# Two memory tiles for the modulation rows, gate blocks of layer 1 loaded in layer 1, a longer warm-up, the last projection in three column ranges, a new order table

## The chip, the core and the metric

One core of one Trainium2 chip runs the whole program. The metric is the device time of one execution in microseconds (us); lower is better. TensorE (PE) multiplies and has a queue of weight loads of its own (PEld in the profile), VectorE (DVE) and ScalarE (ACT) do the elementwise work, and SyncE (SP) issues nearly all transfers (DMA).

## The reference

One inference step with two layers over 640 tokens (512 latent, 128 context), width 1024, all in float32:

```
h = RMSNorm(x) * (1 + scale) + shift      # shift, scale, gate = SiLU(cond) @ ada_w[l] + ada_b[l]
u = h @ w_in[l]                           # one input projection for four head groups
A: differential attention   B: gated short convolution
C: latent attention         D: neighbourhood attention
y = concat(group_out * SiLU(z)) @ w_out[l]
x = x + gate * y                          # after layer 1: final RMSNorm
```

Context and latent tokens have different conditions, so shift, scale and gate exist twice (s = 0, 1). The keys and values of the context tokens are outputs too.

## The kernel before

Activations lie with the 1024 features on partitions, as eight blocks of 128 by 640 tokens. To keep float32 accuracy every product is done three times: an operand is split into an upper and a lower part (`whi`, `wlo` of a weight, `hh`, `hl` of an activation block), and upper by upper, upper by lower and lower by upper are summed in a PSUM bank. Each matmul instruction has its own load of 128 by 128 weights, even where the next one multiplies with the same weights: the trace has 5570 of both.

The code records operations into a plan (class `Plan`). `schedule` (L325) goes over them with a price for each and picks, for each engine, the one that can start first; ties go by a number, the place in the program plus `SHIFT[group]`. The table `SHIFT` so sets the order within each engine's queue. All instructions are emitted from one line, L464; the profile therefore goes by tile names.

The stages, in order of time:

- **Start.** `keep_warm(WARM[0])` puts dummy matmuls of 128 columns (`bank<-ones`) at the head of PE. Eight modulation blocks of layer 0 follow (`ada_first`, L611): each loads two halves of `adaw` (512 KB each) into buffers that are used for other things later (`yt`, `adst`, `qs`, `ks`, `bias`, `hl`), multiplies them with the condition `cs` (four matmuls of 32 columns of weights by 256 for a half, 8 records in the trace), copies the result to `adasb` (ACT), sums it with two tiny matmuls (`bank<-par,adasb`), and DVE writes `modB` and `modA` of that block. `keep_warm(WARM[1..4])` puts dummies behind the first four halves. Next to it runs the RMS norm of the first 384 columns: eight squares on ACT, seven sums on DVE, one matmul with `ones` by 384 columns, Ln and Exp on ACT, then `t<-cst,thi` on DVE. `finish` (L690) scales a block by `modA` and `modB` on ACT and splits it into `hh` and `hl`, with which the input projection `tm_chunk(0, "a")` (L700) begins: per block 5 token tiles by 3 products by 512 columns.
- **Middle.** Projections and attention of layer 0. In between, `ada_next` takes the other sixteen modulation blocks (four gate blocks of layer 0, all twelve of layer 1) one by one: two loads into `wraw`, matmuls, copy, and two small transfers into the DRAM tile `adram`; `ada_end` (L638) reads them back, sums them and writes `modA`, `modB`, `modG`. In the code before, all sixteen are done in layer 0. Then layer 0's output projection and layer 1 in the same manner.
- **Output projection.** `HALVES[l]` cuts the 640 columns into ranges; the loop at L1330 goes over them. For each range, eight output blocks (`fb`) take 24 matmuls each: 8 input blocks by 3 products. The split weights stay in `whi`/`wlo`, `adst`, `qs`/`ks` and `yt` for all ranges. DVE adds `gate * acc` to the old x (`cst<-bank,modG,...`), ACT squares the block (`thi`, `tlo`) and multiplies it by the norm weight. In layer 1 the end of a range is: last sum, square, matmul with `ones`, Ln, Exp, two products with 1/rms on DVE, two transfers to `yt`.

```
HALVES = (((0, 384), (384, 640)), ((0, 384), (384, 640)))   # L26: before, layer 0 and layer 1
WARM = (15, 10, 8, 4, 4)                                    # L36
for hf, (c0, c1) in enumerate(HALVES[l]):                   # L1330
    for n, kt in enumerate(YK):
        PE.matmul(acc[:, :w], wh[:, kt], hh[kt][:, c0:c1], ...)
        PE.matmul(acc[:, :w], wh[:, kt], hl[kt][:, c0:c1], ...)
        PE.matmul(acc[:, :w], wl[:, kt], hh[kt][:, c0:c1], ...)
```

Of the kernel before, what the change touches and what calls it, by code (L numbers as in the profile page):

```python
# [21 lines left out]
L = 2  # L22
X1 = (4, 4, 4, 4, 4, 4, 4, 4)
WA = (2, 6, 11, 16)
LATE = (16, 17)
HALVES = (((0, 384), (384, 640)), ((0, 384), (384, 640)))  # L26
# [9 lines left out]
WARM = (15, 10, 8, 4, 4)  # L36
SHIFT = {"": 38, "a0": 47, "a1": -28, "ada0": -8588, "av0": 6296, "av1": 3, "b0": 25951, "b1": 24557, "c0": -2462, "d0": 62, "d1": 33941, "f0.0": -174, "f0.1": 22, "f1.0": -183, "f1.1": 2841, "h0.0": -4317, "h0.1": 205, "h1.0": 7, "h1.1": -10499, "h10.0": 1418, "h10.1": -8, "h11.0": 638, "h11.1": 4686, "h2.0": -3351, "h2.1": -22079, "h3.0": -2855, "h4.0": -2974, "h4.1": -2909, "h5.0": -1, "h5.1": -9, "h6.0": 797, "h6.1": -6113, "h7.0": 20, "h7.1": 13278, "h8.0": 5300, "h9.0": -7596, "lam": 6901, "o0.0": -505, "o1.0": -80, "o1.1": 26, "p0.0": 162, "p0.1": -20, "p2.0": -2125, "p2.1": 432, "p3.0": -1337, "p3.1": 4371, "p4.0": -1388, "p4.1": -27369, "p7.0": -1727, "p7.1": 960, "p8.1": -18800, "pa0": 51, "pa1": -552, "qk00": -18970, "qk01": 10605, "qk10": 10903, "qk11": 14623, "x0": -3000, "x1": 6892, "x2": -1536, "y0": -1625, "y1": 9425, "y2": -77, "z0": -13, "z1": -227}
FILL = (('z', 4), ('d', 6), ('qk0', 7), ('qk1', 8), ('b', 12))
D = 1024
NT = 640  # L40
# [442 lines left out]
def body(ctx: ExitStack, tc: tile.TileContext, i, o):  # L483
# [68 lines left out]
    for op in R.ops[-WARM[0]:]:  # L552
        op.cost = {"PE": 320}
# [9 lines left out]
    adram = R.tile([L, 12, 2, 4, 256], F32, name="adram", space="dram")  # L563
# [6 lines left out]
    def wpiece(l, name, idx):  # L570
        if l == 0 and name == "a":
            at(WA[idx])
            R.offset += WBOOST
        else:
            R.offset = 0
        off, kk, n = PIECES[name][idx]
        src = i["win"][l, off:off + 128 * kk * n].rearrange("(p c) -> p c", p=128)
        return wsplit(src, kk, n)
# [19 lines left out]

    def ada_rows(l, blk, raws, warm):
# [24 lines left out]

    def ada_block(l, blk):
# [8 lines left out]
        for s in range(2):  # L634
            SP.dma_start(adram[l, blk, s], sb[s:97 + s:32])
        R.need, R.group = need, group

    def ada_end(l, b0, b1_):  # L638
# [3 lines left out]
        tag, n = ("wraw", 1024) if l == 0 else ("bias", BIAS_W)  # L642
        rows = R.tile([128, n], F32, name=tag, tag=tag, bufs=3 if l == 0 else 1)[0:m, 0:1024]
        SP.dma_start(rows, adram[l, b0:b1_].rearrange("b s k c -> (b s) (k c)"))
# [5 lines left out]
        v = pt[:, 0:2 * m].rearrange("p (c b s) -> p b c s", c=2, b=nb)  # L650
        wide = lambda t, n: t[:, :, None].to_broadcast([128, n, 2])
        if nb == 12:
# [3 lines left out]
        for c in range(2):  # L656
            V.tensor_add(modG[:, l, c:8:2], v[:, nb - 4:nb, c], wide(sp[:, l, 16 + c:24:2], 4))
        R.group = group

    later = [(0, b) for b in range(8, 12)] + [(1, b) for b in range(12)]  # L660

    def ada_next(l):

        if l == 0 and later:
            ll, blk = later.pop(0)
            ada_block(ll, blk)
            if blk == 11:
                ada_end(ll, 8 if ll == 0 else 0, 12)
                gate[0] = len(R.ops) - 1
# [166 lines left out]
    for l in range(L):  # L836
        if l == 0:
# [359 lines left out]
        def fill_d():  # L1197
# [5 lines left out]
            ada_next(l)  # L1203
# [4 lines left out]
        def fill_qk(p):  # L1208
# [15 lines left out]
            ada_next(l)  # L1224
# [10 lines left out]
            ada_next(l)  # L1235
# [91 lines left out]
        c0, c1 = HALVES[l][1]  # L1327
        xall = R.tile([128, 2816], F32, name="xall", tag="hl")[:, :8 * (c1 - c0)].rearrange("p (k c) -> p k c", k=8)
        SP.dma_start(xall, xsrc[:, :, c0:c1].rearrange("k p c -> p k c"))
        for hf, (c0, c1) in enumerate(HALVES[l]):  # L1330
            R.group = f"o{hf}.{l}"
            xn = xns[hf]
            for fb in range(8):
# [5 lines left out]
                if hf:  # L1339
                    xo = xall[:, fb]  # L1340
# [17 lines left out]
            rstd = rms_rows(xn, (0, 7, 8) if l + 1 == L and hf == 1 else (0, 8))  # L1358
# [126 lines left out]
```

## Time and profile before

| | us |
|---|---|
| median of 3 runs | 825.73 (825.54 to 825.94) |
| profiled execution | 825.87 |
| its span in the profile | 824.1 |
| PE busy | 799.7 (97%), 5570 matmuls |
| PEld busy | 746.0 (91%) |
| DVE / ACT busy | 578.9 (70%) / 505.0 (61%) |
| mean granted TensorE clock | 0.992 of full |

The 1.8 us between the profiled execution's time and its span lie outside what the trace covers. A matmul's record is longer than the room it takes, since matmuls overlap; what one costs is the distance from its start to the next start. PEclk is the clock that was granted to TensorE: 1.00 is 2.4 GHz, 0.50 is 1.2 GHz.

### The profile page before, as it was taken

How to read it: one execution, taken by the hardware profiler on the slowest of the kernel's cores; microseconds unless marked ns; L12 is line 12 of the kernel's file. 1: busy time of each engine (PE TensorE's matmuls, PEld its weight loads, DVE VectorE, ACT ScalarE, POOL GpSimd, SP SyncE). 2: the span in 40 equal slices, each digit the busy share in tenths (PEclk: the TensorE clock that was granted, in tenths of full speed). 3: DMA queues.
4: the chain of work that ended last, by engine and by line, in shares of the span. 5: the costliest groups of instructions: out<-in, count | busy, mean ns of one | idle time of the engine just before them, and what ended most of it. 6: DMA issues, size and time to landing. Idle time of an engine off the chain costs nothing.

```text
span 824.1 us, 14974 instructions
## 1 busy us (share of the span) xinstructions
PE 799.7 (97%) x5570; PEld 746.0 (91%) x5570; DVE 578.9 (70%) x1296; ACT 505.0 (61%) x1108; POOL 0.2 (0%) x4
## 2 busy tenths in 40 slices
PE   7999999998999999999999999999999999999995
PEld 6789898998898888989998899999999989999995
DVE  3744499798674985837367636986987899876643
ACT  5852487677883874624237436866887878645432
POOL 0000000000000000000000000000000000000000
PEclk8999999999999999999999999999999999999998
DMA  9924533444562787756650355333146646823221
GB/s 313 364 100 109 169 88 83 114 133 119 173 162 83 186 259 203 254 170 215 238 193 30 89 139 165 105 79 104 61 108 159 145 106 184 254 70 90 84 77 52
DMA packets 50029, 120.15 MB, mean 146 GB/s; under 512 B 7940, under 2 KB 21892, under 8 KB 49956
## 3 DMA queue, kind: packets, MB, share of 16 engines
q1 hardware_dynamic: 49812, 119.11, 48.2%
q8 instruction: 44, 0.72, 0.4%
q14 instruction: 29, 0.24, 0.1%
q10 hardware_dynamic: 144, 0.07, 0.0%
HBM read 82.69 MB, written 6.59 MB: 108 GB/s over the span
## 4 chain that ended last, share of the span: by engine, by line
PE 85%; ACT 5%; DVE 4%; DMA 3%; issue 1%; SPq 1%; DVEq 0%; ACTq 0%
PE bank L464 81%; PE pair L464 5%; ACT t L464 2%; ACT thi L464 1%; DVE t L464 1%; DMA wraw<-adaw 1%; DMA bias<-bias 1%; DVE tlo L464 1%; DMA yt<-adaw 1%; SPq L464 1%; DVE mn L464 1%; DMA q<-hl 0%; DVE cst L464 0%; ACT avt L464 0%; DVE adasb L464 0%
## 5 line engine op out<-in xcount | busy, mean ns | idle before, releaser
L464 PE MATMUL bank<-hh,whi 128*128 128x320 f32 (+2 forms) x640 | 202.2, 317 | 0.3 <-ACT adasb L464 0.3
L464 PE MATMUL bank<-hh,wlo 128*128 128x320 f32 (+2 forms) x640 | 201.0, 315 | 0.0
L464 PE MATMUL bank<-hl,whi 128*128 128x320 f32 (+2 forms) x640 | 200.7, 314 | 0.0
L464 PEld LDWEIGHTS bank<-hh,whi 128*128 128x128 f32 x640 | 120.5, 188 | 2.8 <-issue 1.2
L464 PEld LDWEIGHTS bank<-hh,wlo 128*128 128x128 f32 x640 | 120.3, 188 | 2.4 <-issue 1.6
L464 PEld LDWEIGHTS bank<-hl,whi 128*128 128x128 f32 x640 | 120.6, 188 | 2.1 <-issue 1.2
L464 DVE TENSOR_TENSOR wlo<-wraw,whi 128x1024 fp32r<-128x1024 f32 (+1 forms) x64 | 76.5, 1195 | 62.8 <-ACT whi L464 62.5
L464 ACT ACTIVATE thi<-bank 128x512 fp32r<-128x512 f32 (+3 forms) x164 | 76.8, 486 | 49.1 <-PE bank L464 45.4
L464 PE MATMUL bank<-whi,hl 128*128 128x256 f32 (+2 forms) x320 | 105.9, 332 | 0.0
L464 PE MATMUL bank<-whi,hh 128*128 128x256 f32 (+2 forms) x320 | 105.1, 333 | 0.7 <-DVE adst L464 0.5
L464 PE MATMUL bank<-wlo,hh 128*128 128x256 f32 (+2 forms) x320 | 105.1, 329 | 0.0
L464 DVE TENSOR_TENSOR tlo<-bank,thi 128x512 fp32r<-128x512 f32 (+3 forms) x164 | 86.8, 548 | 16.9 <-ACT thi L464 16.1
L464 ACT ACTIVATE whi<-wraw 128x1024 fp32r<-128x1024 f32 (+1 forms) x64 | 66.3, 1035 | 51.9 <-PE bank L464 40.6
L464 DVE TENSOR_REDUCE mn<-pair 128x1 f32<-128x640 f32 x96 | 77.9, 816 | 7.0 <-PE pair L464 4.4
L464 ACT ACTIVATE t<-pair,mn 128x640 f32<-128x640 f32 x96 | 75.9, 792 | 9.2 <-DVE mn L464 6.1
L464 PE MATMUL bank<-par,t 128*128 128x128 f32 x456 | 79.6, 274 | 1.4 <-DVE tlo L464 1.4
L464 PE MATMUL pair<-ks,qs 96*128 96x320 f32 (+1 forms) x256 | 62.9, 327 | 4.6 <-ACT t L464 4.3
L464 PEld LDWEIGHTS bank<-whi,hh 128*128 128x128 f32 x320 | 60.1, 189 | 6.6 <-issue 0.8
L464 PE MATMUL bank<-thi,vs 128*128 128x256 f32 (+3 forms) x224 | 64.3, 295 | 0.8 <-ACT t L464 0.8
L464 PEld LDWEIGHTS bank<-whi,hl 128*128 128x128 f32 x320 | 60.3, 188 | 5.1 <-issue 1.6
L464 PEld LDWEIGHTS bank<-wlo,hh 128*128 128x128 f32 x320 | 60.4, 189 | 5.0 <-issue 1.2
L464 PE MATMUL bank<-tlo,vs 128*128 128x256 f32 (+3 forms) x224 | 64.0, 303 | 0.5 <-DVE tlo L464 0.5
(191 smaller groups left out, 1450.7 us busy)
## 6 DMA issues: line engine op xcount, KB each, us to landing
wraw<-win SPq DMA_DIRECT2D x52, 512.0 KB, 4.1
wraw<-adaw SPq DMA_DIRECT2D x32, 512.0 KB, 4.8
ks<-hl SPq DMA_DIRECT2D x48, 192.0 KB, 3.6
wraw<-wout SPq DMA_DIRECT2D x16, 512.0 KB, 3.9
bias<-bias SPq DMA_DIRECT2D x8, 896.0 KB, 6.8
ks<-hl SPq DMA_DIRECT2D x48, 96.0 KB, 2.2
qs<-hl SPq DMA_DIRECT2D x48, 80.0 KB, 2.1
qs<-hl SPq DMA_DIRECT2D x24, 160.0 KB, 2.5
```

The lines of the kernel that those rows point to most:

```text
L464: done = getattr(engines[op.engine], method)(*[fix(x) for x in args], **{k: fix(x) for k, x in kw.items()})
```

## The change

- `HALVES` of layer 1: three ranges, 384, 128 and 128 columns, in place of 384 and 256. The old x for columns 384 to 640 is still loaded in one transfer (`xall`).
- `WARM`: 34 dummies at the head instead of 15, then 4, 4, 4, 4 instead of 10, 8, 4, 4. The first weight piece's load moves ahead (`WA` 0, 5, 10, 15).
- At the start the second half of block 0's modulation is made to wait for the norm's matmul (`second`, `R.rooted`), the first weight piece's split comes behind the norm, and `modB`/`modA` come earlier on DVE (priority 3000 lower).
- `adram` becomes two tiles, one for each condition s; `ada_end` reads each in a transfer of its own.
- The four gate blocks of layer 1 move from layer 0 to layer 1 (`later` has two lists, and `fill_b` of layer 1 takes from the second); blocks 0 to 7 of layer 1 end in an `ada_end` of their own in layer 0.
- A new `SHIFT` table: nearly every group has another number, so the order changes in all queues.

```
-HALVES = (((0, 384), (384, 640)), ((0, 384), (384, 640)))
+HALVES = (((0, 384), (384, 640)), ((0, 384), (384, 512), (512, 640)))
-WARM = (15, 10, 8, 4, 4)
-SHIFT = {"": 38, "a0": 47, "a1": -28, "ada0": -8588, ...
+WARM = (34, 4, 4, 4, 4)
+SHIFT = {"": 38, "a0": 44, "a1": -51, "ada1": 1198, ...
...
-    adram = R.tile([L, 12, 2, 4, 256], F32, name="adram", space="dram")
+    adram = [R.tile([L, 12, 4, 256], F32, name=f"adram{s}", space="dram") for s in range(2)]
...
+        if l == 0 and name == "a" and idx == 0:
+            R.ops[split_at].deps.add(R.rooted)
...
+            if warm and blk == 0:
+                second.append(len(R.ops))
...
+        for op in R.ops[-2:]:
+            op.prio -= 3000
...
-            SP.dma_start(adram[l, blk, s], sb[s:97 + s:32])
+            SP.dma_start(adram[s][l, blk], sb[s:97 + s:32])
...
-        SP.dma_start(rows, adram[l, b0:b1_].rearrange("b s k c -> (b s) (k c)"))
+        for s in range(2):
+            SP.dma_start(rows[s * nb:s * nb + nb], adram[s][l, b0:b1_].rearrange("b k c -> (b) (k c)"))
...
-    later = [(0, b) for b in range(8, 12)] + [(1, b) for b in range(12)]
+    later = ([(0, b) for b in range(8, 12)] + [(1, b) for b in range(8)], [(1, b) for b in range(8, 12)])
...
+                if n == 0:
+                    R.rooted = len(R.ops) - 1
...
+                    if n == 0 and "PE" in op.calls:
+                        for k in range(4):
+                            R.ops[second[1] + k].deps.add(op.n)
...
-                    xo = xall[:, fb]
+                    xo = xall[:, fb, c0 - HALVES[l][1][0]:c1 - HALVES[l][1][0]]
...
-            rstd = rms_rows(xn, (0, 7, 8) if l + 1 == L and hf == 1 else (0, 8))
+            rstd = rms_rows(xn, (0, 7, 8) if l + 1 == L and hf == 2 else (0, 8))
```

PE's queue at the very start, before. `ones` are the dummies, `yt,cs` halves of modulation blocks, `t_112,ones` the norm's matmul, `par_62,adasb` the small sums, `whi,hh` the first real matmuls:

```order
L464 MATMUL bank<-ones 128x128 x15
L464 MATMUL bank<-yt,cs 32x256 x4
L464 MATMUL bank<-ones 128x128 x4
L464 MATMUL bank<-yt,cs 32x256 x4
L464 MATMUL bank<-ones 128x128
L464 MATMUL bank<-t_112,ones 128x384
L464 MATMUL bank<-par_62,adasb 128x2 x2
L464 MATMUL bank<-yt,cs 32x256 x8
```

The same place in PE's queue after the change:

```order
L464 MATMUL bank<-ones 128x128 x34
L464 MATMUL bank<-yt,cs 32x256 x4
L464 MATMUL bank<-ones 128x128 x4
L464 MATMUL bank<-t_118,ones 128x384
L464 MATMUL bank<-yt,cs 32x256 x4
L464 MATMUL bank<-ones 128x128 x3
L464 MATMUL bank<-par_62,adasb 128x2 x2
L464 MATMUL bank<-yt,cs 32x256 x4
```

The norm's matmul moves ahead of the second half of block 0. From the first `yt,cs` to the last dummy of the start there stand 26 dummies before and 16 after; a row of nine of them, which stood behind the first block's `whi,hh` matmuls, is gone.

PE's queue in layer 1's output projection where the first range ends, before:

```order
L464 MATMUL bank<-hh_536,yt 128x384
L464 MATMUL bank<-hl_542,yt 128x384
L464 MATMUL bank<-hh_536,yt 128x384
L464 MATMUL bank<-hh_203,whi 128x256
L464 MATMUL bank<-hl_222,whi 128x256
L464 MATMUL bank<-hh_203,wlo 128x256
L464 MATMUL bank<-hh_245,whi 128x256
```

The same place after:

```order
L464 MATMUL bank<-hh_558,yt 128x384
L464 MATMUL bank<-hl_570,yt 128x384
L464 MATMUL bank<-hh_558,yt 128x384
L464 MATMUL bank<-hh_213,whi 128x128
L464 MATMUL bank<-hl_237,whi 128x128
L464 MATMUL bank<-hh_213,wlo 128x128
L464 MATMUL bank<-hh_261,whi 128x128
```

192 matmuls of 256 columns become 384 of 128 columns. They stand in one unbroken row to the end of the program, but for the four matmuls with `ones`; no longer matmul stands between them.

## Rows read from the trace of the kernel before

**Rows 1.** The page: busy time of the engines, share of the span, instructions.
```profile
PE 799.7 (97%) x5570; PEld 746.0 (91%) x5570; DVE 578.9 (70%) x1296; ACT 505.0 (61%) x1108; POOL 0.2 (0%) x4
```

**Rows 2.** Stages: window, length, busy of PE, PEld, DVE, ACT, POOL; clock, DMA.
```profile
10.70:20.80 10.10, 10.09 (x76) 6.71 (x76) 3.58 (x9) 4.31 (x9) 0.00 (x0) 0.73 1.01 381
...
100.00:420.00 320.00, 311.70 (x2275) 286.73 (x2274) 234.35 (x530) 204.55 (x459) 0.00 (x0) 1.00 0.56 166
...
790.50:814.20 23.70, 23.70 (x198) 23.40 (x196) 11.34 (x25) 8.75 (x18) 0.00 (x0) 1.00 0.19 68
```

**Rows 3.** The start: start, duration, instruction, idle before; last, landings (issues, KB, median us).
```profile
1.05 5.93 PE L464 MATMUL bank<-ones 128*128 128x128 f32 x30 [1.05 <-DVE ones L464]
10.71 1.08 PE L464 MATMUL bank<-yt,cs 128*32 128x256 f32 x8 [3.74 <-DMA yt<-adaw]
11.72 2.08 PE L464 MATMUL bank<-ones 128*128 128x128 f32 x8
15.33 1.23 PE L464 MATMUL bank<-t,ones 128*128 128x384 f32 x2
16.39 0.50 PE L464 MATMUL bank<-par,adasb 128*128 128x2 f32 x4
20.26 0.64 PE L464 MATMUL bank<-yt,cs 128*32 128x256 f32 x8
20.83 0.96 PE L464 MATMUL bank<-whi,hh 128*128 128x512 f32 x3
23.01 2.17 PE L464 MATMUL bank<-ones 128*128 128x128 f32 x18
28.64 1.61 SPq L464 DMA_DIRECT2D hl<-adaw  x2
42.87 1.07 PE L464 MATMUL bank<-hl,cs 128*32 128x256 f32 x16
...
wraw<-win SPq DMA_DIRECT2D x6, 512.0 KB, 9.8
```

**Rows 4.** Weight loads, then matmuls, of 128 columns in succession.
```profile
340.81 0.19 PEld L464 LDWEIGHTS bank<-thi,vs 128*128 128x128 f32 x1
340.92 0.19 PEld L464 LDWEIGHTS bank<-tlo,vs 128*128 128x128 f32 x1
341.03 0.19 PEld L464 LDWEIGHTS bank<-hh,wlo 128*128 128x128 f32 x1
...
340.86 0.28 PE L464 MATMUL bank<-thi,vs 128*128 128x128 f32 x1
340.98 0.27 PE L464 MATMUL bank<-tlo,vs 128*128 128x128 f32 x1
341.09 0.36 PE L464 MATMUL bank<-hh,wlo 128*128 128x320 f32 x1
```

**Rows 5.** PE: two 128-column matmuls behind a longer one, then others.
```profile
226.88 0.34 PE L464 MATMUL bank<-ks,qs 128*128 128x128 f32 x2
227.06 0.27 PE L464 MATMUL bank<-k,q 128*128 128x128 f32 x1
```

**Rows 6.** The 256-column range: first and last of its 192 matmuls, then the ending.
```profile
790.54 0.28 PE L464 MATMUL bank<-hh,whi 128*128 128x256 f32 x1
...
792.80 0.81 PE L464 MATMUL bank<-thi,ones 128*128 128x384 f32 x2
...
813.85 0.28 PE L464 MATMUL bank<-hh,yt 128*128 128x256 f32 x1
814.17 0.61 DVE L464 SCALAR_TENSOR_TENSOR cst<-bank,modG,hl 128x128 f32<-128x128 f32 x2 [1.29 <-PE bank L464]
815.28 0.70 PE L464 MATMUL bank<-tlo,ones 128*128 128x256 f32 x2 [0.72 <-ACT tlo L464]
816.97 2.36 DVE L464 TENSOR_TENSOR cst<-cst,thi 128x1024 f32<-128x1024 f32 x2 [2.19 <-ACT thi L464]
818.23 1.55 SPq L464 DMA_DIRECT2D yt<-cst  x2
```

More of the change, by code (lines that the diff above doesn't have):

```diff
@@ L23 @@
 X1 = (4, 4, 4, 4, 4, 4, 4, 4)
-WA = (2, 6, 11, 16)
+WA = (0, 5, 10, 15)
 LATE = (16, 17)
-HALVES = (((0, 384), (384, 640)), ((0, 384), (384, 640)))
+HALVES = (((0, 384), (384, 640)), ((0, 384), (384, 512), (512, 640)))
 START = ((0, 384), (384, 640))
@@ L551, in body @@
     keep_warm(WARM[0])
-    for op in R.ops[-WARM[0]:]:
-        op.cost = {"PE": 320}
+    for n, op in enumerate(R.ops[-WARM[0]:]):
+        op.cost = {"PE": 340 if n < 14 else 215}
     modA = R.tile([128, L, 8, 2], F32, name="modA")
@@ L577, in wpiece @@
         src = i["win"][l, off:off + 128 * kk * n].rearrange("(p c) -> p c", p=128)
-        return wsplit(src, kk, n)
+        split_at = len(R.ops) + 1
+        w = wsplit(src, kk, n)
+        if l == 0 and name == "a" and idx == 0:
+            R.ops[split_at].deps.add(R.rooted)
+        return w
     def wsplit(src, kk, n, place=None):
@@ L597, in at @@
         R.offset = ada_at[min(h, 15)] + 7.5 * max(h - 15, 0) + 0.5 - len(R.ops)
+    second = []
     def ada_rows(l, blk, raws, warm):
@@ L641, in ada_end @@
         m = 2 * nb
-        tag, n = ("wraw", 1024) if l == 0 else ("bias", BIAS_W)
-        rows = R.tile([128, n], F32, name=tag, tag=tag, bufs=3 if l == 0 else 1)[0:m, 0:1024]
-        SP.dma_start(rows, adram[l, b0:b1_].rearrange("b s k c -> (b s) (k c)"))
+        tag, n = ("wraw", 1024) if nb == 4 else ("bias", BIAS_W)
+        rows = R.tile([128, n], F32, name=tag, tag=tag, bufs=3 if nb == 4 else 1)[0:m, 0:1024]
+        for s in range(2):
+            SP.dma_start(rows[s * nb:s * nb + nb], adram[s][l, b0:b1_].rearrange("b k c -> (b) (k c)"))
         su = R.tile([128, 256], F32, name="adasb", bufs=1)[0:m]
@@ L649, in ada_end @@
             PE.transpose(pt[:, m * c:m * c + m], su[:, 128 * c:128 * c + 128], ident[0:m, 0:m])
-        v = pt[:, 0:2 * m].rearrange("p (c b s) -> p b c s", c=2, b=nb)
+        v = pt[:, 0:2 * m].rearrange("p (c s b) -> p b c s", c=2, b=nb)
         wide = lambda t, n: t[:, :, None].to_broadcast([128, n, 2])
-        if nb == 12:
+        if nb == 8:
             V.tensor_add(modB[:, l], v[:, 0:8, 0], wide(sp[:, l, 0:8], 8))
@@ L655, in ada_end @@
             V.tensor_mul(modA[:, l], modA[:, l], wide(sp[:, l, 24:32], 8))
-        for c in range(2):
-            V.tensor_add(modG[:, l, c:8:2], v[:, nb - 4:nb, c], wide(sp[:, l, 16 + c:24:2], 4))
+        for c in range(2 if nb == 4 else 0):
+            V.tensor_add(modG[:, l, c:8:2], v[:, :, c], wide(sp[:, l, 16 + c:24:2], 4))
         R.group = group
-    later = [(0, b) for b in range(8, 12)] + [(1, b) for b in range(12)]
+    later = ([(0, b) for b in range(8, 12)] + [(1, b) for b in range(8)], [(1, b) for b in range(8, 12)])
     def ada_next(l):
-        if l == 0 and later:
-            ll, blk = later.pop(0)
+        if later[l]:
+            ll, blk = later[l].pop(0)
+            gate[1] = l
             ada_block(ll, blk)
-            if blk == 11:
-                ada_end(ll, 8 if ll == 0 else 0, 12)
-                gate[0] = len(R.ops) - 1
+            if blk in (7, 11):
+                ada_end(ll, 0 if blk == 7 else 8, blk + 1)
+                if l == 0:
+                    gate[0] = len(R.ops) - 1
     def rms_rows(xv, cuts=(0, 8), wide=False):
@@ L1202, in fill_d @@
             R.need = dst.ops[0]
-            ada_next(l)
+            if l == 0:
+                ada_next(l)
             tm_seq(l, "dv", ev_d)
@@ L1223, in ev_q @@
                 V.scalar_tensor_tensor(lo, acc, 0.125, hi.bitcast(F32), op0=OP.mult, op1=OP.subtract)
-            ada_next(l)
+            if l == 0:
+                ada_next(l)
             fm_mm(wh, wl, ev_q)
@@ L1234, in ev_k @@
                     SP.dma_start(o["sdk"][l, p], st)
-            ada_next(l)
+            if l == 0:
+                ada_next(l)
             fm_mm(wh, wl, ev_k, 256)
@@ L1326, in body @@
         places += [(big2[:, 2 * n], big2[:, 2 * n + 1]) for n in range(2)]
-        c0, c1 = HALVES[l][1]
+        c0, c1 = HALVES[l][1][0], NT
         xall = R.tile([128, 2816], F32, name="xall", tag="hl")[:, :8 * (c1 - c0)].rearrange("p (k c) -> p k c", k=8)
```

2 lines of the change are left out of this document (1 added, 1 removed).

## The prediction

> **What bounds the kernel now.** I read the page first: PE is busy for 799.7 of 824.1 us, the load queue PEld for 746.0, DVE and ACT are far behind [rows 1]. So the end is set by how fast PE gets through its queue, and a change counts for what it does to the distance between matmul starts, or to PE's idle time. The stages come next [rows 2]. From 10.7 to 20.8 us the granted clock averages 0.73. Between 100 and 420 us PE is idle for 8.3 us (320.0 less 311.7). In the last projection, 790.5 to 814.2, it has no idle time, and PEld is busy for 23.4 of 23.7 us: the weight loads there have nothing to spare. The reader should keep that last row in mind; the largest term comes from it.
>
> **The change part by part.**
>
> *Three column ranges.* The 256-column range begins with a matmul at 790.54, and its last one starts at 813.85 [rows 6]. That is 23.3 us for 191 steps; the first range's norm matmul at 792.80, 0.81 long and overlapping its neighbours, takes about 0.6 of it, so a step is 0.119 us and 192 of them 22.8 us. After the change there are 384 matmuls of 128 columns in an unbroken row. What does one cost? A matmul of this size needs few columns, but each brings its own load of 128 by 128 weights. The trace of before has short runs of such matmuls. In [rows 4] the loads start at 340.81, 340.92 and 341.03, so 0.11 us apart, and the matmuls on them at 340.86, 340.98 and 341.09, at the same 0.11 to 0.12. A matmul starts about 0.06 us behind its load, and the next load 0.11 behind the last, whatever the matmul's length. In [rows 5] the first two records last 0.34 us together where one of them lasts 0.27 to 0.28 [rows 4], so the second started only 0.06 to 0.07 after the first: its load had been taken early, under a 320-column matmul. The two starts up to the third matmul take 0.18 us together, so the second step is 0.11 again. One load can be hidden under a long matmul; in a row of 384 short ones there is none to hide under. I take 0.1095 us a step, the loads' rate in [rows 4]: 384 x 0.1095 = 42.0 us, less 22.8, is **+19.2 us**. The ends are 0.06 us (matmuls alone, +0.2 us) and 0.12 us (the slower matmul step in [rows 4], +23.3 us); the value is near the upper end because [rows 4] is the only succession in which no load had a long matmul to run under.
>
> The Trainium skill (TensorE: Matmul & The Clock Gate, section "Back-to-back issue gap") gives a sustained 81 ns for a stream of load and matmul pairs at 128 columns. By that figure the range would take 31.1 us, +8.3 in place of +19.2. The succession in [rows 4] is slower than the Trainium skill has it.
>
> *The ending.* Behind the last projection matmul come one sum, a square, a norm matmul, Ln, Exp, two products and two transfers, from 813.85 to the end at 824.1, so 10.2 us [rows 6]. With 128 columns in place of 256: one of the two sums (0.61 for both) goes, -0.3; the norm matmul (0.70) loses about 0.25; the two products, 2.36 us for 1024 elements each, halve but for a start-up, -1.1; square, Ln and Exp lose about 0.1 each; the transfers at the end carry half the bytes, -0.3. Sum **-2.3 us**, ends -1.5 and -2.8. The middle range ends under the last one's matmuls: it has 192 x 0.11 = 21 us of cover on ACT and DVE, which are busy for 8.8 and 11.3 of 23.7 us in that stage.
>
> *The start.* PE has a gap of 3.74 us ahead of the first modulation half at 10.71, and behind it works at a clock that [rows 2] averages to 0.73. At the low clock a half takes 1.01 us to the next start (10.71 to 11.72), later 0.57 (20.26 to 20.83): 0.44 saved on each of two. Four dummies there last 2.08 us, 0.52 each; nine at the high clock last 2.17, 0.24 each, so the five low ones cost 1.4 too much. The norm's matmul takes 1.06 (15.33 to 16.39), half of which goes. Sum 2.8 us [rows 3]. The 15 dummies of the opening end at 1.05 + 5.93 = 6.98, 19 further ones at 0.24 bring that to 11.5, 0.8 behind 10.71: that goes off, 2.0 remain. Further, 26 dummies behind the opening become 16, and the row of nine at 23.01 held the queue while the first block was done: 10 x 0.24 = 2.4. Moving the norm ahead brings Ln, Exp and the first scaled block forward by some 2 us, so that real matmuls stand where the dummies were; this is the cover without which the 2.4 would be idle time instead. What limits it is the transfers: the DMA works at a share of 1.01 [rows 2]. The last two modulation halves are issued from 28.64 to 30.25; loads of that size land 9.8 us after their issue in this stretch, so about 38.4 and 40, and PE uses them at 42.87 [rows 3]. PE comes 3 to 4 us late to them, so it can move forward by about that before it meets the data. I take **-4.4 us** (2.0 + 2.4), ends -1 (transfers take over) and -5.5.
>
> *Gate blocks of layer 1, two memory tiles, new order.* The same 16 blocks, matmuls and 512 KB loads are done; four move from a stage where PE idles for 8.3 us in 320 to layer 1, where the weight buffers `wraw` now have 4 MB more to pass. On SP two small reads replace one, twice, and the reads of one more `ada_end`: a few issues, not on PE's path while the result is needed hundreds of matmuls later. The most that an order could gain there is those 8.3 us [rows 2]; no row shows what a worse order costs. I take half of it to either side: **0, ends -4 and +4**.
>
> Sum: +19.2 - 2.3 - 4.4 + 0 = +12.5 us. The profiled execution took 825.87 us, 0.14 above the median of 825.73 and 1.8 above its span; nothing in the change touches what lies outside the span. 825.9 + 12.5 = **838.4 us**.
>
> **The rivals.**
>
> *Loads hide (faster).* If PEld could run ahead by more than one load, matmuls would go at their own pace of 0.06 us and the three ranges would cost +0.2: 825.9 + 0.2 - 6.7 = 819.4. For it: the short step in [rows 5]. Against: the step behind it is 0.11 again, and in [rows 4] every one is. It decides below (22.8 + 6.7) / 384 = 0.077 us a step: under that the program is faster than before.
>
> *Loads half hidden (slower, a little).* If every second load were taken early in a long row too, the mean step would be that of [rows 5], 0.09 us: 384 x 0.09 = 34.6, +11.8, total 831.0. Against it: the early load there had a 320-column matmul to run under. By the 81 ns of the Trainium skill's section named above it would be 827.5.
>
> *The start's gain meets the transfers (slower than forecast).* With -1 in place of -4.4 the total is 841.8. For it: the DMA share of 1.01 in that stretch. Against: PE is the later one at 42.87. It is within the range.
>
> *The clock falls in the last projection.* With matmuls at half the loads' pace PE's array rests for half the time. If the clock went to 1.2 GHz and loads with it, a step would be some 0.22 us and the total near 880. For it: [rows 2] show a stretch at the low level behind an idle gap. Against: here there is no gap, and all stages from 100 us on show 1.00.
>
> **How the numbers follow.** Forecast (loads bound the last projection): 0.82, half hidden 0.06, hidden 0.08, clock 0.04. The forecast's own range is 825.9 + 12.5 with the ends of start and middle, about 833 to 844 (their ends need not fall together); the third rival is inside it. I reach down to 831 to take in the half-hidden case, and leave out the hidden case and the clock: range 831 to 844.5. A measurement of this kernel can tell about 0.2%, 1.7 us. Faster by more than that: the hidden case, 0.08. Within it: a half-hidden step near 0.08, 0.02. Slower: 0.90.
>
> **What the profile after would show.** Right: loads in the two last ranges start 0.11 us apart, PEld busy throughout, the projection's last two ranges take about 42 us; the first modulation half runs at clock 1.00, the row of nine dummies is gone and the last modulation halves are used before 40 us; from the last projection matmul to the end some 8 us. Wrong: steps of 0.06 there would sink the forecast whatever the rest does. A PE gap ahead of the last projection, waiting for `wraw` loads of weights, would put the middle's term at its upper end.

## The result, and the profile after

The changed kernel takes 831.37 us (median of 4 runs, 830.72 to 831.47), the kernel before 825.63 beside it: a ratio of 1.0071, interval 1.0054 to 1.0088. It is slower by 5.7 us, where the forecast was 12.7 us. The profiled execution took 831.45 us with a span of 829.7, which is 5.6 longer than before's 824.1.

The page of after (busy us, share, instructions), to be held against [rows 1]:

```profile
PE 816.9 (98%) x5784; PEld 766.4 (92%) x5784; DVE 582.0 (70%) x1304; ACT 508.9 (61%) x1128; POOL 0.2 (0%) x4
```

PE and its loads have become busier by 17 and 20 us: 214 more matmuls, 214 more loads. The stages of after, in the columns of [rows 2]:

```profile
0.00:10.70 10.70, 9.66 (x68) 9.66 (x68) 4.35 (x13) 6.57 (x12) 0.20 (x4) 1.00 0.80 265
10.70:20.80 10.10, 10.10 (x89) 6.92 (x88) 6.28 (x16) 6.26 (x13) 0.00 (x0) 1.00 0.99 346
100.00:420.00 320.00, 317.61 (x2331) 299.70 (x2330) 245.47 (x557) 211.96 (x461) 0.00 (x0) 1.00 0.54 159
...
778.90:822.50 43.60, 43.60 (x389) 43.34 (x388) 14.59 (x34) 13.16 (x36) 0.00 (x0) 1.00 0.15 49
822.50:829.70 7.20, 1.03 (x7) 0.65 (x6) 1.64 (x3) 1.39 (x4) 0.00 (x0) 0.64 0.27 73
```

The stretch from 10.7 to 20.8 us now has the clock at 1.00, its upper level, in place of 0.73. Between 100 and 420 us PE's idle time is 2.4 us, not 8.3. The last two column ranges fill 43.6 us in which the loads are busy for 43.34, and 7.2 us follow to the end.

PE at the places of [rows 3] and [rows 6] in after (start, duration, instruction, idle before it):

```profile
1.04 9.90 PE L464 MATMUL bank<-ones 128*128 128x128 f32 x68 [1.04 <-DVE ones L464]
10.87 0.64 PE L464 MATMUL bank<-yt,cs 128*32 128x256 f32 x8
11.44 1.16 PE L464 MATMUL bank<-ones 128*128 128x128 f32 x8
...
18.96 0.50 PE L464 MATMUL bank<-whi,hh 128*128 128x512 f32 x1
...
40.61 1.07 PE L464 MATMUL bank<-hl,cs 128*32 128x256 f32 x16
...
778.91 0.22 PE L464 MATMUL bank<-hh,whi 128*128 128x128 f32 x1
778.97 0.27 PE L464 MATMUL bank<-hl,whi 128*128 128x128 f32 x1
779.08 0.28 PE L464 MATMUL bank<-hh,wlo 128*128 128x128 f32 x1
...
822.49 0.28 PE L464 MATMUL bank<-hh,yt 128*128 128x128 f32 x1
```

The weight loads in the same range of after:

```profile
799.88 0.19 PEld L464 LDWEIGHTS bank<-hh,yt 128*128 128x128 f32 x1
799.99 0.19 PEld L464 LDWEIGHTS bank<-hl,yt 128*128 128x128 f32 x1
800.10 0.30 PEld L464 LDWEIGHTS bank<-hh,yt 128*128 128x128 f32 x2
```

Loads start 0.11 us apart and matmuls keep that distance; only the very first step, 778.91 to 778.97, is 0.06, since its load ran under a matmul of 384 columns. From 778.91 to 822.49 there are 383 steps in 43.58 us, 0.114 each, the four norm matmuls among them.

So the 5.6 us of span fall into four parts. The start: the last 512-column matmul of layer 0's first projection begins at 57.99 in place of 61.65, -3.7. The middle: the first 128- or 256-column matmul of the last projection begins at 778.91 in place of 790.54, -11.6, so -8.0 beyond the start. The last ranges: 43.6 us for 23.3, +20.3. The ending: 7.2 us for 10.2, -3.0. The sum is +5.6. Three of these are near the forecast. The middle, forecast at 0, is not, and most of the runs below ask about it. Its two stretches, before and then after, in the columns of [rows 2]:

```profile
61.65:790.54 728.89, 718.15 (x5008) 679.07 (x5007) 531.24 (x1185) 455.75 (x1004) 0.00 (x0) 1.00 0.48 139
...
57.99:778.91 720.92, 715.84 (x5010) 679.29 (x5009) 532.84 (x1185) 455.83 (x1006) 0.00 (x0) 1.00 0.49 141
```

PE's idle time in them falls from 10.7 to 5.1 us, which is 5.7 of the 8.0; the other 2.3 are shorter steps. Nearly all of the idle time won lies in layer 0: up to the last matmul of its output projection (439.60 and 421.90) it falls from 8.9 to 2.9 us, behind it it goes from 1.8 to 2.1.

Each of these marks comes from one execution. Seven traces of these runs, before's among them, have before's PE list up to the 512-column mark, and put that matmul at 60.63 to 62.16 us; five have after's list up to there, and put it at 57.31 to 58.45. So the start's 3.7 us are good to about 1 us, and the means of the two groups, 61.4 and 58.1, say 3.3.

### The profile page after: what moved, and what is told of

The parts are those of the page before. It is cut to its first block, busy times and chain, and to the rows that moved or that the text cites. A ratio compares the mean times of both kernels' runs of the same rounds, so it can differ in the third digit from the quotient of the medians.

```text
span 829.7 us, 15448 instructions
## 1 busy us (share of the span) xinstructions
PE 816.9 (98%) x5784; PEld 766.4 (92%) x5784; DVE 582.0 (70%) x1304; ACT 508.9 (61%) x1128; POOL 0.2 (0%) x4
## 4 chain that ended last, share of the span: by engine, by line
PE 83%; DMA 6%; DVE 3%; SPq 3%; ACT 3%; issue 1%; DVEq 0%; ACTq 0%
PE bank L464 78%; PE pair L464 6%; SPq L464 3%; DMA bias<-adaw 1%; ACT t L464 1%; DMA cst<-xt 1%; DMA wraw<-wuq 1%; DMA wraw<-win 1%; DMA adst<-adaw 1%; DMA yt<-adaw 1%; DMA wraw<-adaw 1%; ACT whi L464 1%; DVE wlo L464 1%; DVE adasb L464 0%; DVE cst L464 0%
## 5 line engine op out<-in xcount | busy, mean ns | idle before, releaser
L464 PE MATMUL bank<-hl,whi 128*128 128x320 f32 (+3 forms) x656 | 206.1, 314 | 0.1
L464 PE MATMUL bank<-hh,wlo 128*128 128x320 f32 (+3 forms) x656 | 206.2, 315 | 0.0
L464 PE MATMUL bank<-hh,whi 128*128 128x320 f32 (+3 forms) x656 | 206.1, 315 | 0.0
L464 PEld LDWEIGHTS bank<-hl,whi 128*128 128x128 f32 x656 | 123.7, 189 | 3.0 <-issue 2.1
L464 PEld LDWEIGHTS bank<-hh,wlo 128*128 128x128 f32 x656 | 123.7, 189 | 3.0 <-issue 1.6
L464 PEld LDWEIGHTS bank<-hh,whi 128*128 128x128 f32 x656 | 123.6, 189 | 2.0 <-issue 0.8
L464 ACT ACTIVATE thi<-bank 128x512 fp32r<-128x512 f32 (+3 forms) x164 | 75.8, 486 | 45.4 <-PE bank L464 43.6
L464 PE MATMUL bank<-par,t 128*128 128x128 f32 x456 | 77.6, 274 | 0.9 <-DVE tlo L464 0.9
```

The costliest lines, as they stand in the source:

```text
L464: done = getattr(engines[op.engine], method)(*[fix(x) for x in args], **{k: fix(x) for k, x in kw.items()})
```

## Experiments: the three ranges

**Two ranges again**, the rest of the change kept:

```diff
-HALVES = (((0, 384), (384, 640)), ((0, 384), (384, 512), (512, 640)))
+HALVES = (((0, 384), (384, 640)), ((0, 384), (384, 640)))
-            rstd = rms_rows(xn, (0, 7, 8) if l + 1 == L and hf == 2 else (0, 8))
+            rstd = rms_rows(xn, (0, 7, 8) if l + 1 == L and hf == 1 else (0, 8))
```

> The changed kernel with the last output in two column ranges (384 and 256) again, everything else of the change kept. Theory one (each matmul of 128 columns lasts as long as the load of its weights, 0.112 us in the trace of after, and the three ranges are the only part that costs): the last 384 steps of 0.112 us (43.6 us) become 192 of 0.119 and the ending grows by the 3.0 us that it had shrunk, so 831.4 - 20.3 + 3.0 = 814.1 us. Theory two (the ranges cost little by themselves, and the time went because the new order or the longer start left the last projection worse fed): the time stays above 825 us, and the last projection of 256 columns shows steps clearly above 0.12 us.

Measured: 812.95 us, a ratio to before of 0.9858 (0.9844 to 0.9873), near the 814.1 of theory one. It is faster than both kernels, and 18.4 us of the changed kernel's time hang on the third range. The rest of the change gains 12 us.

**Three ranges alone**, on the kernel before (HALVES, the two lines on `xall`, the condition on `hf`).

> The kernel before with the last output in three ranges and nothing else of the change. Theory one (loads set the pace of 128-column matmuls): 825.6 + 20.3 - 3.0 = 842.9 us, with steps of 0.11 us in the last two ranges. Rival (the loads hide here, and it is something else in after that stretches the steps): steps near 0.06 us and 819 to 822 us.

Measured: 846.24 us, ratio 1.0260 (1.0240 to 1.0279), 3.3 us above theory one's figure. The last two ranges run from 789.87 to 833.23, 43.4 us, as in after. But the ending did not shrink: it takes 11.7 us (833.2 to 844.9) where after takes 7.2. PE, then DVE and ACT, at this kernel's end:

```profile
833.34 0.44 PE L464 MATMUL bank<-thi,ones 128*128 128x128 f32 x2
837.55 0.80 PE L464 MATMUL bank<-thi,ones 128*128 128x128 f32 x2 [3.78 <-DVE thi L464]
...
834.41 0.29 DVE L464 TENSOR_TENSOR thi<-thi,tlo 128x128 f32<-128x128 f32 x1 [0.52 <-ACT thi L464]
834.62 0.69 DVE L464 TENSOR_TENSOR cst<-cst,thi 128x512 f32<-128x512 f32 x1
835.22 0.28 DVE L464 TENSOR_TENSOR thi<-thi,tlo 128x128 f32<-128x128 f32 x1
835.42 0.69 DVE L464 TENSOR_TENSOR cst<-cst,thi 128x512 f32<-128x512 f32 x1
836.02 1.48 DVE L464 TENSOR_TENSOR thi<-thi,tlo 128x128 f32<-128x128 f32 x4
...
833.81 0.37 ACT L464 ACTIVATE thi<-bank,epst 128x128 f32<-128x128 f32 x1 [12.54 <-PE bank L464]
834.08 0.30 ACT L464 ACTIVATE thi<-cst 128x128 f32<-128x128 f32 x1
```

The row sums of the last range (`thi,tlo`) are all done behind the last projection matmul, mixed with the products of the middle range (`cst,thi`), and PE waits 3.78 us for them. The ACT row shows what held them up. The `thi,ones` matmul at 833.34 is the norm of the middle range, and in PE's queue it stands behind the last projection matmul. ACT's Ln on its result (`thi<-bank,epst`) stands in ACT's queue ahead of squares of the last range, so ACT is idle for 12.54 us and those squares come behind it. In after the middle range's norm matmul starts at 803.51, among the last range's matmuls, and the sums are done as the columns come, one each 2.7 us:

```profile
817.45 0.35 DVE L464 SCALAR_TENSOR_TENSOR cst<-bank,modG,hl 128x128 f32<-128x128 f32 x1 [1.66 <-PE bank L464]
818.17 0.29 DVE L464 TENSOR_TENSOR thi<-thi,tlo 128x128 f32<-128x128 f32 x1 [0.38 <-ACT tlo L464]
820.13 0.35 DVE L464 SCALAR_TENSOR_TENSOR cst<-bank,modG,hl 128x128 f32<-128x128 f32 x1 [1.66 <-PE bank L464]
820.86 0.29 DVE L464 TENSOR_TENSOR thi<-thi,tlo 128x128 f32<-128x128 f32 x1 [0.38 <-ACT tlo L464]
```

DVE and ACT had the time for it in both kernels; what differs is the order. The old table has an entry for `f1.1` (2841, which moves the group back), made for the last range, which now falls on the middle one, and none for `f2.1`. That these entries do it is read from the tables, not tried one by one. The prediction had the middle range end "under the last one's matmuls" by the cover on DVE and ACT alone; the cover was there, and without the new table nothing used it.

**Wider ranges**, to tell a pace set by loads from one set by columns:

```diff
-HALVES = (..., ((0, 384), (384, 512), (512, 640)))
+HALVES = (..., ((0, 288), (288, 464), (464, 640)))
```

> The changed kernel with its three last ranges cut at 288 and 464 columns, so that the last two have 176 columns each instead of 128, with as many matmuls and weight loads. If the load of the weights sets the step (theory one), 176 columns take the same 0.112 us as 128: the first range falls from 192 x 0.174 to about 192 x 0.132 us (-8 us), the other two stay at 43 us, the ending grows by under 1 us, in all about 823 to 824 us. If a narrow matmul simply runs at half speed per column (rival), the steps go to 0.112 x 176 / 128 = 0.154 us, +16 us, and the time to about 839 us. If neither counts and columns set the step, 0.08 us and about 811 us.

Measured: 824.65 us, ratio to before 1.0001 (0.9989 to 1.0014), against 823 to 824 of theory one. PE, the first matmuls of 176 columns in that kernel:

```profile
771.97 0.24 PE L464 MATMUL bank<-hh,whi 128*128 128x176 f32 x1
772.05 0.27 PE L464 MATMUL bank<-hl,whi 128*128 128x176 f32 x1
772.16 0.27 PE L464 MATMUL bank<-hh,wlo 128*128 128x176 f32 x1
772.28 0.28 PE L464 MATMUL bank<-hh,whi 128*128 128x176 f32 x1
772.39 0.27 PE L464 MATMUL bank<-hl,whi 128*128 128x176 f32 x1
```

The first step is 0.08 us, since its load ran under a matmul of 288 columns: so much a matmul of 176 columns takes when it need not wait for a load. The others are 0.11 us, as with 128 columns; over all 383 of them, norm matmuls included, 0.1136 against 0.1138. Forty-eight more columns cost nothing, and the rival of half speed per column would have shown 0.154. The loads, which start a median 0.112 us apart in both kernels, set the pace. This kernel also gives the point from which they stop doing so: its 288-column range has steps of 0.1328 us, after's 384-column range 0.1760, so 0.00045 us a column; on that line 0.112 us is reached at about 242 columns, an estimate from these two rows. The 256-column range of before lay just above it.

## Experiments: where the middle's 8 us come from

**The table alone**, on the kernel before:

```diff
-SHIFT = {"": 38, "a0": 47, "a1": -28, "ada0": -8588, "av0": 6296, ...
+SHIFT = {"": 38, "a0": 44, "a1": -51, "ada1": 1198, "av0": 16706, ...
```

> The kernel before with the order table of after and nothing else. It asks where the 8 us come from that after gains between the start and the last projection. Theory T (the table orders the middle better): 825.6 - 8 = about 818 us, TensorE's idle time in 100 to 420 us falls from 8.3 us to under 4. Theory G (the gain comes from moving four modulation blocks out of the first layer): the table alone gives nothing or, made for another plan, costs: 824 to 830 us, idle time in 100 to 420 us still 6 us or more.

Measured: 839.37 us, ratio 1.0180 (1.0160 to 1.0200). Both theories missed; PE's idle time in the middle about doubles, from 10.7 to 20.3 us. PE between the layers in this kernel, where it idles longest:

```profile
442.35 0.30 PE L464 MATMUL bank<-par,adasb 24*128 24x24 f32 x2 [3.87 <-DVE adasb L464]
443.78 1.22 PE L464 MATMUL bank<-thi,ones 128*128 128x256 f32 x2 [1.13 <-DVE thi L464]
445.62 0.79 PE L464 MATMUL bank<-whi,hh 128*128 128x512 f32 x1 [0.61 <-ACT hh L464]
```

The first row transposes the 24 modulation rows of layer 1. In the old plan all 12 blocks have to be done by here, four of them more than in the plan the table was made for, and with this table they come late: layer 1's first matmul waits for them. The table is not a better order; it is an order for another plan. So the parts were run in all their combinations, on the kernel before with two ranges: T the table, M the modulation part (two memory tiles, gate blocks moved), S the start.

**M alone** (with `ada_next`, `ada_end` and `adram` as in the change):

```diff
-    later = [(0, b) for b in range(8, 12)] + [(1, b) for b in range(12)]
+    later = ([(0, b) for b in range(8, 12)] + [(1, b) for b in range(8)], [(1, b) for b in range(8, 12)])
```

> The kernel before with the modulation part of the change alone: two memory tiles, and the four gate blocks of layer 1 loaded in layer 1 (layer 0 then computes 12 blocks beside its attention, not 16); old order table, old start, two output ranges. Theory G (taking four blocks out of the first layer frees it, whatever the table): 825 - 8 = about 817 us, TensorE idle in 100 to 420 us down from 8.3 us to about 3. Theory P (table and blocks belong together; each alone disturbs the order): no gain, 824 to 835 us, as the table alone gave 839.

**M and T** (both edits):

> The kernel before with the modulation part and the new order table, old start and two output ranges: what the two together give without the start. If the gain of 8 us in the middle belongs to this pair, 825 - 8 = 817 us, and the start's 3.6 us stand apart (813 with it). If the pair works only behind the new start, since the table was made for it: above 820 us.

**S alone** (with `second`, `rooted` and the priority of the first modulation results as in the change):

```diff
-WA = (2, 6, 11, 16)
+WA = (0, 5, 10, 15)
-WARM = (15, 10, 8, 4, 4)
+WARM = (34, 4, 4, 4, 4)
```

> The kernel before with the start alone: 34 warm-up matmuls, the second modulation half held behind the first row sums, the earlier transfers, the earlier finish of the modulation. If the start is a term of its own (theory one): the last matmul of the first 512-column projection comes at about 58.0 instead of 61.65 us, and the time is 825 - 3.6 = 821.3 us. Rival: the start's gain needs the new table, which moves the finishing steps of the first layer's input too; then 824 us or more.

**S and M:**

> The kernel before with the start and the modulation part, old order table, two output ranges. It is the kernel of 813 us less the table. Theory G: 825 - 8 - 3.6 = 813.5 us, and the table is worth nothing by itself. Theory P: 821 to 832 us, and the missing 8 us and more are what the table gives once the blocks have been moved.

**S and T:**

> The kernel before with the start and the new order table, but all 16 blocks in layer 0; it is the kernel of 813 us less the modulation part, and the last of the eight combinations of start, table and modulation part. Theory P (the table fits only the plan with the blocks moved): 839.4 - 3.6 = about 836 us. Rival (the table needs the new start, and the blocks matter little): below 822 us.

| parts | us | ratio to before | interval |
|---|---|---|---|
| none (before) | 824.9 | 1 | |
| T | 839.37 | 1.0180 | 1.0160 to 1.0200 |
| M | 829.07 | 1.0060 | 1.0038 to 1.0081 |
| S | 822.07 | 0.9972 | 0.9957 to 0.9988 |
| S, M | 826.78 | 1.0024 | 1.0010 to 1.0038 |
| S, T | 836.76 | 1.0135 | 1.0119 to 1.0152 |
| M, T | 818.50 | 0.9928 | 0.9907 to 0.9949 |
| S, M, T (the two-range kernel) | 812.95 | 0.9858 | 0.9844 to 0.9873 |

S gives 2.3 to 2.9 us beside anything but M and T together, where it gives 5.5. Alone it also falls short of its theory in the trace: its last 512-column matmul starts at 59.13, not at 58.0; with T it starts at 58.41, so a part of the start's gain needs the table. T costs 14.4 us and M 4.1 by themselves; together they gain 6.5. That is no sum of two prices but a fit of one to the other: theory G fell with the row of M, theory P stood. The pair also works behind the old start, if by less.

**The tiles alone**, on the kernel before, all 16 blocks in layer 0:

```diff
-        SP.dma_start(rows, adram[l, b0:b1_].rearrange("b s k c -> (b s) (k c)"))
+        for s in range(2):
+            SP.dma_start(rows[s * nb:s * nb + nb], adram[s][l, b0:b1_].rearrange("b k c -> (b) (k c)"))
```

> The kernel before with the modulation rows through two memory tiles (and read back in two transfers) and nothing else: all 16 blocks stay in layer 0. It asks whether the 4 us that the modulation part cost by itself come from the tiles or from the blocks. Theory one (the blocks): 825 us, within 1.5. Rival (the tiles and the second transfer): 828 to 830 us.

Measured: 833.78 us, ratio 1.0111 (1.0096 to 1.0126). Two small transfers more, and 8.8 us are lost, beyond what either theory had. The trace says where: up to layer 1's first projection the kernel keeps near before's times (468.76 against 468.05 at its last 512-column matmul), and the last projection's first range ends 7.8 us later (798.14 against 790.37). The tiles are used in layer 0; the loss is in layer 1, in which no row of the modulation is moved.

**Tiles with the old order.** The planner is shown one tile, as before, and the two tiles are put in when its instructions are written out. So every list stands as in before, but for the reading transfers, which are two instead of one, twice:

```diff
+                elif t.tag == "adram":
+                    t.tile = [pools["dram"].tile([L, 12, 4, 256], F32, name=f"adram{s}", ...) for s in range(2)]
...
+                for s in range(2):
+                    done = engines[op.engine].dma_start(rows[s * nb:s * nb + nb], args[1].root.tile[s][l, bs]...)
```

> The modulation rows go through two memory tiles and come back in two transfers each time, but every other instruction of every engine stands where it stands in the kernel before (the planner sees one tile, as before; only the two readings become two transfers each). The tiles alone with the order that the planner then made had cost 8.8 us. Theory O (that was the order, which a small change of the plan reshuffles): 825 us, within 1.5. Rival (the tiles and their transfers cost something on the chip): 830 us or more.

Measured: 825.68 us, ratio 1.0005 (0.9994 to 1.0017). The tiles cost nothing. The 8.8 us were the plan that the planner made once it had one more reading transfer to place, twice.

**Nudges.** If that is so, a plan changed for no reason should cost as well. One constant in the planner's estimates is changed by 0.5 to 1.3%, and nothing in what is computed:

```diff
-SLOW, LATER = 1.1, 800
+SLOW, LATER = 1.1, 810
```
```diff
-SLOW, LATER = 1.1, 800
+SLOW, LATER = 1.11, 800
```
```diff
-    LAG = {("PE", "PE"): 0, ("PE", "ACT"): 200, ...
+    LAG = {("PE", "PE"): 0, ("PE", "ACT"): 201, ...
```

> The kernel before with one constant of the planner's estimate of a transfer changed by about one per cent (800 to 810 ns until a landed transfer counts as done). The work is the same instruction for instruction; only the order differs, in 928 lines of TensorE's list. Theory O (the table was fitted to one exact plan, and any reshuffle loses some of the fit): slower than before, by 3 to 10 us. Rival (reshuffles scatter both ways around 825): 822 to 828 us.

> The kernel of 813 us with another constant of the planner's estimate changed by one per cent (the factor on a transfer's duration, 1.10 to 1.11). The same work in another order. Theory O: slower, 816 to 823 us, so that about as much as the middle's gain of 8 us is given back by a change that does nothing else. Rival (the gain belongs to the blocks that were moved, and survives a reshuffle): 812 to 815 us.

> The kernel of 813 us with the planner's estimate of the way from TensorE to ScalarE at 201 ns, not 200. The same work in another order. Theory O: slower, 816 to 823 us. Rival (the gain belongs to the moved blocks): 812 to 815 us.

> The nudge of the kernel of 813 us that gave 822.3 us (the planner's factor on a transfer's duration, 1.10 to 1.11), on the kernel before. It and the next run ask whether anything of the middle's gain belongs to the moved blocks. Theory M (an exact fit is worth some 8 us in either plan, and moving the blocks some 6 us beside it): 829 to 833 us, so that the unfitted plans differ by as much as the fitted ones. Theory F (only the fit counts, and the kernel before was fitted less well): the unfitted plans differ by the start alone, so 822 + 3.6 = about 825 to 827 us.

> The nudge that gave 820.9 us on the kernel of 813 us (the estimate of the way from TensorE to ScalarE at 201 ns, not 200), on the kernel before; its order differs from before in 255 lines of TensorE's list. Theory M: 828 to 833 us. Theory F: 824 to 826 us.

| nudge | on before, us (interval of the ratio to before) | on the two-range kernel, us (same interval) |
|---|---|---|
| none | 825.0 | 812.95 (0.9844 to 0.9873) |
| 800 to 810 | 831.39 (1.0050 to 1.0077) | not run |
| 1.10 to 1.11 | 826.62 (1.0011 to 1.0035) | 822.34 (0.9944 to 0.9970) |
| 200 to 201 | 824.05 (0.9972 to 1.0004) | 820.92 (0.9926 to 0.9951) |

On the two-range kernel the two nudges give back 9.4 and 8.0 us: about all that the middle had gained. On before one costs 6.3, one 1.9, one nothing.

"Only the order differs" is true of PE, whose instructions are the same to the last one. Some elementwise operations can go to VectorE or to ScalarE, however, and the planner picks. DVE has 1296 instructions in before and 1288, 1296 and 1315 with the nudges in the order of the table, 1295 in the two-range kernel and 1286 and 1310 with its two; `tiles_alone` has 1289. So order and choice of engine changed together, and no run takes them apart. The choice alone is no account of the losses: the nudge to 201 moves some 15 to 20 operations to DVE in either kernel, and costs 8.0 us in one and nothing in the other.

The stage rows of the two-range kernel and, under them, of its first nudge, from 640 to 700 us in layer 1's attention:

```profile
640.00:700.00 60.00, 59.84 (x433) 55.10 (x432) 51.47 (x143) 43.91 (x109) 0.00 (x0) 1.00 0.67 191
...
640.00:700.00 60.00, 57.54 (x412) 52.04 (x412) 51.94 (x139) 49.76 (x120) 0.00 (x0) 1.00 0.60 164
```

In these 60 us the nudged kernel gets 21 matmuls fewer through PE, at the same clock, with 2.3 us more idle time, and ACT is busy for 5.9 us more (the two windows don't hold quite the same piece of the program). The rest shows as longer steps. This can be summed over the whole run: give every matmul the short step of its shape (the tenth percentile over the steps of before, the two-range kernel and their nudges), and the sum is 671.5 to 672.2 us in each of them. What differs is the steps that last over 0.15 us longer than that. Their excess is 56.8 us in before, 62.1 with 810, 41.9 in the two-range kernel, 50.2 and 47.4 in its nudges. PE's own work is the same; the plan decides how often something is late for it. PE's waits from 100 to 420 us, in before and then in the two-range kernel:

```profile
PE pair L464 <- ACT t L464: 3.4, 3, 1.4
PE bank L464 <- DVE tlo L464: 1.3, 3, 0.6
PE bank L464 <- DMA wraw<-adaw: 0.9, 1, 0.9
...
PE pair L464 <- ACT t L464: 1.4, 1, 1.4
PE bank L464 <- DVE tlo L464: 0.7, 1, 0.7
```

A pair of banks for scores waits for ACT's pass over the last ones (`t`) three times in before and once in the two-range kernel. One gap in before also belonged to a modulation block whose 512 KB came 0.9 us late.

What stays open is whether the moved blocks are worth anything by themselves. With the same nudge the two plans differ by 4.3 and 3.1 us, which is the start's 2.3 to 2.9 and little more; theory M asked for about 7 and over. But the nudges on before cost little, so those two plans are not equally unfitted, and two pairs are few. The runs show that the table with M is worth 6.5 us and that a nudge takes as much away; not that some other order would not win it for the old plan too.

## Experiments: the start

**Fifteen warm-up matmuls**, on the two-range kernel:

```diff
-WARM = (34, 4, 4, 4, 4)
+WARM = (15, 4, 4, 4, 4)
```

> The kernel of 813 us (all of the change but the three ranges) with 15 warm-up matmuls at the start again, not 34. The prediction put 2.0 of the start's gain on the clock that is at its upper level when the first modulation half comes. If so: the granted clock is low again in 10.7 to 20.8 us, the last matmul of the first 512-column projection comes near 60.1 instead of 58.1 us, and the time is about 815 us. Rival (that stretch waits for its transfers, so the clock in it is free): within 0.5 us of 813.

**More dummies**, on the two-range kernel:

```diff
-WARM = (34, 4, 4, 4, 4)
+WARM = (34, 10, 8, 4, 4)
```

> The kernel of 813 us with 10 and 8 dummy matmuls behind the first two modulation halves again, not 4 and 4. The prediction put 2.4 us of the start's gain on the dummies taken away. If so: about 815.4 us, the last matmul of the first 512-column projection near 60.5 us. Rival (they fill time in which the transfers are awaited): 813 us.

Measured: 815.36 and 814.87 us (ratios to before 0.9883, 0.9868 to 0.9898, and 0.9880, 0.9864 to 0.9897) against 812.95, so +2.4 and +1.9 us; the intervals of the ratios just touch that of 812.95. By the times alone both terms look right; the traces say otherwise of the first. PE and the stage row with the short warm-up:

```profile
1.05 6.36 PE L464 MATMUL bank<-ones 128*128 128x128 f32 x30 [1.05 <-DVE ones L464]
10.62 1.08 PE L464 MATMUL bank<-yt,cs 128*32 128x256 f32 x8 [3.22 <-DMA yt<-adaw]
11.63 2.08 PE L464 MATMUL bank<-ones 128*128 128x128 f32 x8
...
10.70:20.80 10.10, 10.10 (x81) 6.86 (x82) 5.41 (x13) 4.99 (x11) 0.00 (x0) 0.85 1.01 371
```

The gap of 3.22 us and the low clock behind it are back, 0.85 on average; the first modulation half takes 1.01 us to the next start (10.62 to 11.63), where after has 0.57. The first 512-column matmul comes 1.6 us later for it, at 20.09 in place of 18.52. But at the last one only 0.3 us are left: 58.44 against 58.12, and 58.44 lies within the 57.31 to 58.45 of the five traces named with the result. The two-range kernel had lost most of the rest in between. Its PE waits up to 60 us, and with the short warm-up there is no wait on `adst` at all:

```profile
PE bank L464 <- DVE ones L464: 1.0, 1, 1.0
PE bank L464 <- DMA adst<-adaw: 1.0, 2, 0.6
```

So the rival holds for most of it: whoever is earlier waits for the transfers, and the clock was worth 0.3 us at 58 us in this pair of traces. Given their spread it may be nothing or about 1 us, but not 2.0. Of the 2.8 us by which this run's span is longer, 2.3 come about at one place far behind the start, on DVE in layer 0's attention:

```profile
324.40 0.56 DVE L464 CUSTOM_DVE_ANT_0 t<-bank,bias 128x384 f32<-128x384 f32 x1 [3.06 <-DMA bias<-bias]
```

The order of every engine is that of the two-range kernel but for the dummies; there the same transfer, issued at 314.20, was in time for its use at 321.24, and here, issued at 315.05, it was awaited until 324.40. Whether the warm-up has any part in that, or whether this execution met a late transfer by chance, the runs don't tell; the four executions took 814.22, 814.66, 816.06 and 816.40 us, and the profiled one is the 816.06. With more dummies the loss is where it should be: the last 512-column matmul at 59.74 in place of 58.12, +1.6 us, and outside the 57.31 to 58.45.

## Why the forecast came out as it did

- **Three ranges, +19.2 forecast: +20.3.** Right in mechanism and size. The loads' rate in [rows 4], taken from three loads in a row, held for 384 of them (0.1095 in the sum, 0.112 measured between loads); the ends of that term, 0.2 and 23.3, enclose it. The wider ranges show that it is the loads. The Trainium skill (TensorE: Matmul & The Clock Gate, section "Back-to-back issue gap") has 81 ns a pair at 128 columns; measured are 114, and the measurement decides. The Trainium skill (the same page, section "LDWEIGHTS (loading the stationary operand)") gives a load of 128 columns 128 / 1.2 ns, 107; the 110 to 112 ns between loads lie 3 to 5% above that.
- **Ending, -2.3: -3.0.** Near, 0.2 us beyond its end of -2.8. What carried it was not the shorter operations alone: in the three ranges with the old table it was +1.5.
- **Start, -4.4: -3.7 at 58 us.** Right in size, not in its split, so the size is in part luck. The dummies taken away, forecast 2.4, showed 1.6 at 58 us; the clock, forecast 2.0, showed 0.3, since the transfers took it back, as the prediction had it for a larger gain. Some 1.8 us (an estimate, with the spread of about 1 us in each mark) are then left for what the sum had no term of its own for, the norm's matmul moved ahead, the modulation results finished earlier and the new table; those were not undone one by one at this place. The last modulation halves are used at 40.61, 2.3 us earlier, where "before 40" was expected.
- **Gate blocks, tiles and order, 0 with ends -4 and +4: -8.0.** This is the step that failed, and it is the whole of the miss: 12.5 forecast from the profile, 5.6 found, 6.9 apart, of which the middle makes 8.0 and the other three together 1.1 the other way. The prediction saw 8.3 us of PE idle time between 100 and 420 us, called that the most an order could gain, and put the term at nothing by taking half of it to either side. In its place the runs show that this order, with the blocks it was made for, won most of that idle time: 5.9 us of the 8.3, and over the whole middle 5.7 us of idle time and 2.3 of shorter steps. What it won is still below the 8.3; at fault are the value 0 and the end of -4. A table that comes with a change can be expected to be made for it, and the table without the blocks (+14.4) and the blocks without the table (+4.1) show that this one was. In the other direction the idle time was no guide at all: the end of +4 was passed by two nudges on the two-range kernel (+9.4, +8.0), one on before (+6.3) and the replanned tiles (+8.8), and in the middle of these four runs idle time rose by 5.6, 3.4, 1.1 and 1.6 us only. Steps can grow without a gap: those of before sum to 814.6 us, 143 over the 671.5 of their short steps, of which 15 are idle time.
- **The total.** 831.37 us lies inside the stated range of 831 to 844.5, and that is luck. The range reached down to 831 for loads half hidden, which were not found; the forecast's own range began at about 833.
- **Rivals.** Loads hidden or half hidden: no, each step is at the loads' rate. The clock in the last projection: 1.00 throughout. The transfers at the start: they took most or all of the clock's share, not the dummies'.

## What to carry to other kernels

Before cutting a matmul's columns, set its step beside the time of its weight load: here 128 by 128 weights take 0.112 us, and below about 242 columns (the estimate above) a narrower cut only adds loads. An order table belongs to the plan it was made for; take the parts of a change apart with the order held fixed, as with the tiles here. What a replanned order may cost is told by nudges (here from nothing to 9.4 us, 1.2%) better than by PE's idle time. The best kernel of these runs is the change without its third range, 812.95 us.

## What the runs showed of the hardware that was not expected

A matmul of 176 columns costs what one of 128 does, 0.1136 and 0.1138 us in a row of 384, as long as each brings its own load of 128 by 128 weights. Two matmuls in succession on the same `wh` weights bring two loads: there are 5784 loads for 5784 matmuls in after. And one transfer of 896 KB, issued at the same point of the same order in two kernels, was in use 7.0 us after its issue in one trace and awaited for 9.3 in the other (314.20 to 321.24, 315.05 to 324.40). Why is not shown. The executions of one kernel differ by 0.5 us in one case (812.69 to 813.20, two ranges) and by 8.4 us in another (819.16 to 827.53, the nudge to 201 on before), so one profiled execution can't settle a question of 1 or 2 us.
